# A transformer pair on one core: the second score pass of 64-wide heads over 128 contraction rows

## The chip, the cores and the metric

The kernel runs on one core of one Trainium2 chip. The metric is the device time of one execution in microseconds (us). Engines are named as in the profile: PE is TensorE's matmuls, PEld its weight loads (they can lie beside matmuls), DVE is VectorE, ACT ScalarE, POOL GpSimd, SP the queue from which nearly all DMAs are issued. The kernel before took 3671.49 us, the median of three runs between 3670.39 and 3673.18 us.

## What is computed

Two transformer blocks on 512 tokens (`S`) of 1024 features; block 2 has two layers, and its first layer also carries 256 context tokens (`C`). Both blocks have attention branches with heads of 64 features, and the change touches those:

```python
# block 1: 8 heads with a mixture of dilated windows, 8 heads on a 2-D neighbourhood, both of the form
s = einsum(q, k) * 64 ** -0.5 + bias          # masked
o = softmax(s) @ v
# block 2, in each of two layers, three branches
def mla(...):  ...                            # 8 heads of 96 features: not touched
def diff_attend(q, k, v, lam):                # 8 heads, two maps of 64 features each
    s = einsum('bqhmd,bkhmd->bhmqk', q * (DIFF_HD ** -0.5), k)
    p = softmax(s.astype(float32), axis=-1)
    a = p[:, :, 0] - lam * p[:, :, 1]
    return einsum('bhqk,bkhd->bqhd', a, v)
# sliding window with sinks: 16 query heads and 4 key heads of 64 features
p = softmax(concatenate([sink, q @ k_window, q @ k_ctx]))
# q and k of diff and of the window branch are rotated first:
def apply_rope(x, cos, sin):
    x1, x2 = halves(x)
    return concatenate([x1 * cos - x2 * sin, x2 * cos + x1 * sin])
```

Each branch is gated and merged; a feed-forward part with a short convolution ends block 1. All is in float32 accuracy.

## The kernel before

**Products in three passes.** To keep float32 accuracy, each operand of a large matmul is split into `hi` (rounded for the fast matmul mode) and `lo` (the rest), and a product is made as hi·hi + hi·lo + lo·hi. Projections do so in lines 338 to 340 and 369 to 371, the values' products in line 665, the scores of the 96-wide `mla` heads in lines 1151 to 1153. Each split costs one ACT instruction for hi and one DVE instruction for lo: `split`, lines 380 to 385. Weights are split on the way in (lines 274 and 275).

**64-wide heads.** Two heads a and b share a projection of 128 features, which stand on 128 partitions. A "page" (`hl`) is a tile of 128 partitions by 2 planes by all tokens. For queries `stack_q` builds, with three partition-to-partition DMAs from a split on 128 partitions, the planes [hi a; lo a] and [lo b; hi b]. For keys `stack_k` builds [hi a; hi a] and [hi b; hi b] with three DMAs; the keys' lo stays as it was split, a on the lower 64 partitions and b on the upper. `products` then needs two passes instead of three. Line 1158 contracts over 128 partitions: hi and lo of q with hi of k. Line 1160 is the second pass, hi of q with lo of k, and contracts over 64 partitions alone:

```python
rw = slice(64 * par, 64 * par + 64)
mm(ps, q[:, par, q_], k[:, par, k_], start=st[0], stop=False)      # L1158
mm(ps, q[rw, par, q_], kl[rw, k_], start=False, stop=st[1])        # L1160
```

**Order of the work.** The program is built by generators. `attend` emits, for each unit of a head (two tiles of 128 queries), the transposes of the unit before, then the scores and the softmax, then filling work: first the preparation of the next head (its projections, `mand`), then the gates' projections (`opt`). A scheduler of the tile framework then moves instructions within each engine's queue; it is why other matmuls stand between two score matmuls. Each engine takes its own queue in order. A matmul with 512 columns that moves at the ordinary pace starts 0.227 us after the one before it.

**Rotation.** `rope64` (line 1377) copies a projection out of PSUM (ACT, line 1386), swaps 32-row quarters with four DMAs (line 1388), multiplies on POOL and DVE and adds (lines 1389 to 1391), then splits. Context tokens are not rotated and are split straight from PSUM. Block 2 has 8 query projections of `diff` and 8 of the window branch in each layer, 32 in all, and 8 + 2 key projections in each layer, 20 in all. Block 1 has 8 query and 8 key projections with 64-wide heads.

Of the kernel before, what the change touches and what calls it, by code (L numbers as in the profile page):

```python
# [9 lines left out]
F32 = mybir.dt.float32  # L10
# [3 lines left out]
ALU = mybir.AluOpType  # L14
# [29 lines left out]
def _units():  # L44
    """Weight units in the order in which the kernel reads them: name, width, layout."""
# [103 lines left out]
def _vec_layout():  # L149
    """Columns of the per-feature vectors: name -> (first column, count)."""  # L150
# [17 lines left out]
def _consts():  # L168
    """Arrays that depend on shapes alone."""
# [9 lines left out]
    # neighbourhood masks: query p = (row, col in 16), key = (chunk, row, col in 16)  # L179
# [9 lines left out]
    # rotary tables: positions on the free axis  # L189
# [27 lines left out]
def _prep(i):  # L217
    """The arrays that are sent: inputs rearranged, and constants of the shapes."""
# [14 lines left out]
    # neighbourhood bias, [(row, col), (chunk of 16 columns - own + 1, row, head, col)] for four heads each;  # L233
    # column offsets outside of the table (all masked) repeat its edge
# [44 lines left out]
class Prog:  # L279
# [15 lines left out]
    # tiles ---------------------------------------------------------------  # L295
# [30 lines left out]
    # products ------------------------------------------------------------  # L326
# [3 lines left out]
    def load_ahead(self, names):  # L330
        """Bring in the first columns of units before the program comes to them."""
# [10 lines left out]
    def proj(self, name, x, evac, kn=KD, m=P, ctx=False, k0=0, off=0, back=False, ranges=None):  # L342
        """evac(PSUM, columns) of w^T x for m columns, x as pages. A generator: yields the tensor engine's ns."""
# [13 lines left out]
    def v_natural(self, name, x, evac, pairs, kn=KD):  # L357
        """evac(pair of token chunks, PSUM [128, 2 * 256]): tokens on partitions, 256 columns."""
# [18 lines left out]
    def split(self, dst_h, dst_l, src, scale=None):  # L377
        """hi and lo of src (times a power of two)."""
# [11 lines left out]
    # order of the program --------------------------------------------------  # L390
# [5 lines left out]
    def run_pairs(self, gens, n=2):  # L396
        """n by n, in turns: what comes in chunk by chunk is used as it comes."""
# [1337 lines left out]
```

## Time and profile before

| what | value |
|---|---|
| median of three runs | 3671.49 us |
| lowest and highest run | 3670.39, 3673.18 us |
| span of the profiled execution, first to last instruction | 3673.4 us |
| PE busy, PE loads busy | 97%, 81% of the span |
| DVE, ACT, POOL busy | 63%, 48%, 10% |
| mean granted TensorE clock | 0.985 of full speed |
| DMA engines busy, mean | about 35% |

The profiled execution has no time of its own beside its span; the span is 0.2 us above the slowest of the timed runs and 1.9 us above their median, so what lies around it is no more than that. Matmuls are pipelined: the busy time of one covers the time from its start to its modelled end, and the next one starts before that end. How fast a row of matmuls goes is therefore read from the distance between their starts, not from their durations.

### The profile page before, as it was taken

What the parts mean: (1) busy time and instruction counts of PE and PEld (TensorE: products, weight loads), DVE (VectorE), ACT (ScalarE), POOL (GpSimd) and SP (SyncE); (2) the same over time, 40 slices, a digit from 0 to 9 for tenths busy, and PEclk for the clock granted to TensorE, in tenths of its full rate; (3) what the DMA queues carried; (4) which work ended last, traced back from release to release, by engine and by line L of the source; (5) the groups of instructions that cost most, each with busy time, mean ns of one, the idle gap of its engine ahead of it and who ended that gap; (6) DMA issues with size and microseconds to landing.
All of it is one profiled execution on the core that took longest, in us unless ns stands there. A gap on an engine that the chain in (4) does not pass through costs nothing. (4 is left out here: it accounts for less than half of the span.)

```text
span 3673.4 us, 54517 instructions
## 1 busy us (share of the span) xinstructions
PE 3559.9 (97%) x19696; PEld 2968.1 (81%) x19696; DVE 2330.0 (63%) x4961; ACT 1773.1 (48%) x4102; POOL 373.0 (10%) x272
## 2 busy tenths in 40 slices
PE   6999998899999999999999999999999999999998
PEld 4777786677888898888888888888888888787777
DVE  7766689963445546556655667655565566647775
ACT  3445443333456524444434667425673444537772
POOL 3001045420001100001000001000010001000010
PEclk9999999999999999999999999999999999999999
DMA  6843455544221153222243222433114332253224
GB/s 228 260 134 111 149 165 181 176 145 133 72 65 31 44 155 81 86 70 73 65 122 126 71 63 57 126 107 88 60 50 143 100 91 77 70 166 91 72 75 138
DMA packets 203232, 396.35 MB, mean 108 GB/s; under 512 B 26865, under 2 KB 40433, under 8 KB 202962
## 3 DMA queue, kind: packets, MB, share of 16 engines
q1 hardware_dynamic: 202258, 389.17, 35.1%
q0 software_dynamic: 704, 3.70, 0.3%
q8 instruction: 155, 2.54, 0.3%
q14 instruction: 115, 0.94, 0.1%
HBM read 302.82 MB, written 38.83 MB: 93 GB/s over the span
## 5 line engine op out<-in xcount | busy, mean ns | idle before, releaser
L338 PE MATMUL mm<-h,whi 128*128 128x512 f32 (+2 forms) x2764 | 1023.2, 370 | 16.5 <-ACT whi L274 11.5
L339 PE MATMUL mm<-h,wlo 128*128 128x512 f32 (+2 forms) x2764 | 1008.2, 365 | 13.1 <-POOL wlo L275 10.5
L340 PE MATMUL mm<-h,whi 128*128 128x512 f32 (+2 forms) x2764 | 1007.7, 365 | 0.1
L274 ACT ACTIVATE whi<-wraw 128x512 fp32r<-128x512 f32 (+1 forms) x763 | 470.0, 622 | 605.9 <-PE mm L340 423.2
L275 DVE TENSOR_TENSOR wlo<-wraw,whi 128x512 fp32r<-128x512 f32 (+2 forms) x675 | 471.1, 704 | 386.8 <-ACT whi L274 376.8
L338 PEld LDWEIGHTS mm<-h,whi 128*128 128x128 f32 (+1 forms) x2764 | 529.0, 191 | 105.3 <-ACT whi L274 16.2
L339 PEld LDWEIGHTS mm<-h,wlo 128*128 128x128 f32 (+1 forms) x2764 | 529.2, 191 | 85.7 <-POOL wlo L275 15.2
L340 PEld LDWEIGHTS mm<-h,whi 128*128 128x128 f32 (+1 forms) x2764 | 528.9, 191 | 75.2 <-issue 3.4
L382 DVE TENSOR_TENSOR ptl<-t,pth 128x512 fp32r<-128x512 f32 (+1 forms) x480 | 298.5, 622 | 178.2 <-ACT pth L381 174.3
L381 ACT ACTIVATE pth<-t 128x512 fp32r<-128x512 f32 (+1 forms) x480 | 260.6, 543 | 270.2 <-PE t L647 265.8
L647 PE MATMUL t<-ident,p 128*128 128x128 f32 x1680 | 283.4, 278 | 12.5 <-DVE ptl L382 7.1
L647 PEld LDWEIGHTS t<-ident,p 128*128 128x128 f32 x1680 | 198.9, 141 | 65.4 <-DVE ptl L382 22.9
L338 PE MATMUL mm<-hl,whi 128*128 128x512 f32 (+1 forms) x680 | 241.8, 356 | 3.1 <-ACT hl L381 2.1
L339 PE MATMUL mm<-hl,wlo 128*128 128x512 f32 (+1 forms) x680 | 240.8, 354 | 0.0
L665 PE MATMUL pv<-pth,hl 128*128 128x256 f32 (+1 forms) x1184 | 223.1, 292 | 4.6 <-ACT pth L381 3.9
L665 PEld LDWEIGHTS pv<-pth,hl 128*128 128x128 f32 x1184 | 178.7, 190 | 44.0 <-ACT pth L381 27.6
L1389 POOL TENSOR_TENSOR st<-st,tab 128x512 f32<-128x512 f32 x52 | 75.1, 1445 | 1245.7 <-DMA st<-st 1034.0
L1160 PE MATMUL s<-hl,hl 64*128 64x256 f32 (+2 forms) x640 | 191.9, 372 | 0.0
L340 PE MATMUL mm<-f,whi 128*128 128x512 f32 (+1 forms) x504 | 178.4, 355 | 0.0
L1179 DVE TENSOR_REDUCE m<-s 128x1 f32<-128x512 f32 x192 | 130.3, 687 | 69.2 <-PE s L1160 52.8
L1158 PE MATMUL s<-hl,hl 128*128 128x256 f32 (+2 forms) x640 | 172.6, 342 | 1.2 <-ACT p L1557 1.2
L275 POOL TENSOR_TENSOR wlo<-wraw,whi 128x512 fp32r<-128x512 f32 x88 | 146.6, 1687 | 254.6 <-ACT whi L274 149.0
(266 smaller groups left out, 6208.5 us busy)
## 6 DMA issues: line engine op xcount, KB each, us to landing
wraw<-in_wst SPq DMA_DIRECT2D x734, 256.0 KB, 2.7
mraw<-in_w_mod SPq DMA_DIRECT2D x48, 512.0 KB, 3.7
hl<-hl SPq DMA_DIRECT2D x116, 192.0 KB, 2.8
mraw<-in_w_ada SPq DMA_DIRECT2D x36, 512.0 KB, 4.9
tg<-st SPq DMA_DIRECT2D x64, 256.0 KB, 2.0
st<-st SPq DMA_DIRECT2D x208, 64.0 KB, 2.0
hl<-hl SPq DMA_DIRECT2D x96, 128.0 KB, 2.3
p<-tg SPq DMA_DIRECT2D x40, 256.0 KB, 2.9
```

The source lines that it names most:

```text
L274: nc.scalar.activation(hi[:, :n], raw[:, :n], AF.Copy)
L275: p.lo.tensor_tensor(lo[:, :n], raw[:, :n], hi[:, :n].bitcast(F32), op=ALU.subtract)
L338: mm(ps, wh, xh, start=first, stop=False)
L339: mm(ps, wl, xh, start=False, stop=False)
L340: mm(ps, wh, xl, start=False, stop=last)
L381: nc.scalar.activation(dst_h, src, AF.Copy)
L382: nc.vector.tensor_tensor(dst_l, src, dst_h.bitcast(F32), op=ALU.subtract)
L647: self.nc.tensor.transpose(tp[:, o + i * P:o + i * P + P], pp[t][:, cols[i]:cols[i] + P], self.ident)
L665: mm(dst, sv, x_[:, o:o + w], start=first, stop=last)
L1158: mm(ps, q[:, par, q_], k[:, par, k_], start=st[0], stop=False)
L1160: mm(ps, q[rw, par, q_], kl[rw, k_], start=False, stop=st[1])
L1179: nc.vector.tensor_reduce(out=m[:, t:t + 1], in_=a[t], axis=AX.X, op=ALU.max, negate=True)
```

## The change

Queries are no longer split on 128 partitions and then moved: `put_q` writes hi and lo of each head directly where they belong, with two ACT and two DVE instructions over 64 partitions each, the DVE ones writing to the other 64 partitions than they read. For keys the lo is stacked like the hi, in a page of its own ([lo a; lo a] and [lo b; lo b]), with three more DMAs. The second pass then contracts over all 128 partitions, [hi; lo] of q with [lo; lo] of k; it so adds the product lo·lo, which was left out before.

```diff
-    def stack_q(self, pg, lp, n):
-        dma(pg[64:, 1, :n], pg[64:, 0, :n])
-        dma(pg[:64, 1, :n], lp[64:, :n])
-        dma(pg[64:, 0, :n], lp[:64, :n])
+    def put_q(self, pg, src, cs, scale):
+        for r, o, c in ((slice(0, 64), slice(64, P), 0), (slice(64, P), slice(0, 64), 1)):
+            hi = pg[r, c, cs]
+            nc.scalar.activation(hi, src[r], AF.Copy, scale=scale)
+            nc.vector.scalar_tensor_tensor(pg[o, c, cs], src[r], scale, hi.bitcast(F32), op0=ALU.mult,
+                                           op1=ALU.subtract)
-    def stack_k(self, pg, n):
+    def stack_k(self, pgs, n):
+        for pg in pgs:
+            dma(pg[64:, 1, :n], pg[64:, 0, :n])
+            dma(pg[:64, 1, :n], pg[64:, 0, :n])
+            dma(pg[64:, 0, :n], pg[:64, 0, :n])
...
     def products(self, qs, ks, jobs):
-        rw = slice(64 * par, 64 * par + 64)
...
-            mm(ps, q[rw, par, q_], kl[rw, k_], start=False, stop=st[1])
+            mm(ps, q[:, par, q_], kl[:, par, k_], start=False, stop=st[1])
...
             def ev_q(ps, cs):      # neighbours
-                hv = own(q[:, 0])
-                nc.scalar.activation(hv, fwd(ps), AF.Copy, scale=0.125)
-                for c in range(4):
-                    nc.vector.scalar_tensor_tensor(own(lo[:, 0])[:, c], fwd(ps)[:, c], 0.125, hv[:, c].bitcast(F32),
-                                                   op0=ALU.mult, op1=ALU.subtract)
-                self.stack_q(q, lo[:, 0], S)
+                qt = self.st()
+                nc.scalar.activation(own(qt), fwd(ps), AF.Copy)
+                self.put_q(q, qt, cs, 0.125)
...
-        klo = self.page()          # window branch
-        kps = [(self.page(), klo[:, g]) for g in range(2)]
+        kps = [(self.page(), self.page()) for g in range(2)]
...
-            q, lo = st["q", j], _ = self.page(), self.page()
+            q = st["q", j] = self.page()
```

The order on three engines is shown at the second `diff` head of layer 0, whose queries' page is `hl_12703` before and `hl_12719` now, the keys' hi page `hl_12704` and `hl_12720`, the keys' lo page `hl_12705` and `hl_12721`.

ACT, the conversion of that head's queries, before (line 384 writes hi on 128 partitions, of the context's 256 columns and of the 512 rotated ones):

```order
L384 ACTIVATE hl_12703<-mm_12808 128x256
L274 ACTIVATE whi_13130<-wraw_13128 128x512
L381 ACTIVATE pth_12863<-t_12858 128x512
L381 ACTIVATE pth_12872<-t_12867 128x512
L384 ACTIVATE hl_12703<-st_12796 128x512
```

The same place now (line 1132 is `put_q`'s hi; the exponentials' lines are one lower):

```order
L1132 ACTIVATE hl_12719<-mm_12826 64x256
L274 ACTIVATE whi_13150<-wraw_13148 128x512
L1132 ACTIVATE hl_12719<-mm_12826 64x256
L381 ACTIVATE pth_12880<-t_12875 128x512
L381 ACTIVATE pth_12889<-t_12884 128x512
L1132 ACTIVATE hl_12719<-st_12812 64x512 x2
```

Two instructions became four, each with as many columns as before and half the partitions; DVE's line 1133 follows them in the same way.

SP, the DMAs of the same head, before (line 1132 is `stack_q`, line 1139 `stack_k`, line 1388 the rotation's swap of the keys, line 266 weights, line 1209 a gate that is parked):

```order
L1132 DMA hl_12703<-hl_12703 64x768
L1132 DMA hl_12703<-hl_12705 64x768
L1388 DMA st_12946<-st_12945 32x512
L1132 DMA hl_12703<-hl_12705 64x768
L1388 DMA st_12946<-st_12945 32x512 x3
L266 DMA wraw_13390<-in_wst 128x512
L266 DMA wraw_13417<-in_wst 128x512
L1139 DMA hl_12704<-hl_12704 64x768 x2
L1209 DMA tg_2520_11773<-st_13039 128x512
L1139 DMA hl_12704<-hl_12704 64x768
```

The same place now (line 1138 is `stack_k`, line 1387 the swap):

```order
L1387 DMA st_12963<-st_12962 32x512 x4
L266 DMA wraw_13411<-in_wst 128x512
L266 DMA wraw_13438<-in_wst 128x512
L1138 DMA hl_12720<-hl_12720 64x768 x2
L1138 DMA hl_12721<-hl_12721 64x768 x2
L1138 DMA hl_12720<-hl_12720 64x768
L1208 DMA tg_2524_11785<-st_13059 128x512
L1138 DMA hl_12721<-hl_12721 64x768
```

The three DMAs of the queries are gone, and the swap of the keys is no longer between them; the keys have six instead of three.

PE, the second map's scores in a unit of that head, before (`mm` is a projection of values that fills; `s_13553` and `s_13554` are the scores of two query tiles with x's keys, `s_13555` those with the context's):

```order
L1158 MATMUL s_13553<-hl_12704,hl_12703 128x512
L1160 MATMUL s_13553<-hl_12705,hl_12703 128x512
L371 MATMUL mm_13477<-whi_13480,h_1080_4552 128x256
L369 MATMUL mm_13477<-whi_13583,h_1081_4553 128x256
L370 MATMUL mm_13477<-wlo_13584,h_1081_4553 128x256
L371 MATMUL mm_13477<-whi_13583,h_1081_4553 128x256
L369 MATMUL mm_13477<-whi_13583,h_1082_4554 128x256
L1158 MATMUL s_13554<-hl_12704,hl_12703 128x512
L1160 MATMUL s_13554<-hl_12705,hl_12703 128x512
L1158 MATMUL s_13555<-hl_12704,hl_12703 128x256 x2
L1160 MATMUL s_13555<-hl_12705,hl_12703 128x256 x2
```

And now (`s_13577` to `s_13579` are the same scores, lines 1157 and 1159 the two passes):

```order
L1157 MATMUL s_13577<-hl_12720,hl_12719 128x512
L1159 MATMUL s_13577<-hl_12721,hl_12719 128x512
L369 MATMUL mm_13667<-whi_13504,h_1084_4564 128x256
L370 MATMUL mm_13667<-wlo_13505,h_1084_4564 128x256
L371 MATMUL mm_13667<-whi_13504,h_1084_4564 128x256
L369 MATMUL mm_13667<-whi_13607,h_1085_4565 128x256
L370 MATMUL mm_13667<-wlo_13608,h_1085_4565 128x256
L371 MATMUL mm_13667<-whi_13607,h_1085_4565 128x256
L1157 MATMUL s_13578<-hl_12720,hl_12719 128x512
L1159 MATMUL s_13578<-hl_12721,hl_12719 128x512
L1157 MATMUL s_13579<-hl_12720,hl_12719 128x256 x2
L1159 MATMUL s_13579<-hl_12721,hl_12719 128x256 x2
```

The passes still alternate, with the same filling work between them; here the whole group stands some 22 rows later in PE's queue than before. The size at a row's end is that of the output, so the 64 contraction rows of line 1160 don't show in it.

## Rows read from the trace of the kernel before

**Rows 1.** The page: span, and busy time of the engines.

```profile
span 3673.4 us, 54517 instructions
...
PE 3559.9 (97%) x19696; PEld 2968.1 (81%) x19696; DVE 2330.0 (63%) x4961; ACT 1773.1 (48%) x4102; POOL 373.0 (10%) x272
```

**Rows 2.** What PE's matmuls waited for, the two longest: total us, times, longest.

```profile
PE mm L338 <- ACT whi L274: 11.5, 7, 3.3
PE mm L339 <- POOL wlo L275: 10.5, 13, 1.3
```

**Rows 3.** Score matmuls by form: out<-in, shape, count | busy, mean ns | idle before.

```profile
L1160 PE MATMUL s<-hl,hl 64*128 64x256 f32 x400 | 100.6, 321 | 0.0
...
L1160 PE MATMUL s<-hl,hl 64*128 64x512 f32 x160 | 72.0, 480 | 0.0
...
L1153 PE MATMUL s<-hl,hl 128*128 128x512 f32 x64 | 25.1, 398 | 0.0
...
L1153 PE MATMUL s<-hl,hl 128*128 128x256 f32 x80 | 22.7, 283 | 0.0
```

**Rows 4.** PE in order of time around scores of `diff`: start us, us, what.

```profile
1704.55 0.39 PE L339 MATMUL mm<-h,wlo 128*128 128x512 f32 x1
1704.77 0.39 PE L1158 MATMUL s<-hl,hl 128*128 128x512 f32 x1
1705.09 0.49 PE L1160 MATMUL s<-hl,hl 64*128 64x512 f32 x1
1705.51 0.50 PE L340 MATMUL mm<-h,whi 128*128 128x512 f32 x1
1705.85 0.40 PE L338 MATMUL mm<-h,whi 128*128 128x512 f32 x1
1706.09 0.40 PE L339 MATMUL mm<-h,wlo 128*128 128x512 f32 x1
```

**Rows 5.** PE in the three-pass scores of `mla`, in order of time.

```profile
1003.89 0.39 PE L1153 MATMUL s<-hl,hl 128*128 128x512 f32 x1
1004.12 0.39 PE L1152 MATMUL s<-hl,hl 128*128 128x512 f32 x1
```

**Rows 6.** PE's weight loads in the stretch of rows 4.

```profile
1704.55 0.19 PEld L1158 LDWEIGHTS s<-hl,hl 128*128 128x128 f32 x1
1705.09 0.18 PEld L1160 LDWEIGHTS s<-hl,hl 64*128 64x128 f32 x1 [0.35 <-issue]
```

**Rows 7.** All matmuls of line 1160: count, ns min/median/max, first and last start.

```profile
L1160 PE MATMUL s<-hl,hl x640: 271/381/792, 84.3 to 3555.7; 64*128 64x512 f32 x72, 64*128 64x256 f32 x64, 64*128 64x384 f32 x24
```

**Rows 8.** Line 1160 in the first stretch: length, PE busy (count), PEld busy, clock, DMA.

```profile
80.00:400.00 320.00, 29.57 (x64) 11.89 (x64) 0.98 0.55 167
```

**Rows 9.** Conversions on ACT and DVE by form.

```profile
L385 DVE SCALAR_TENSOR_TENSOR hl<-st,hl 128x512 fp32r<-128x512 f32 x32 | 21.9, 686 | 5.5 <-ACT hl L384 4.9
...
L384 ACT ACTIVATE hl<-st 128x512 fp32r<-128x512 f32 x32 | 20.2, 631 | 67.1 <-DVE st L1391 67.0
...
L382 DVE TENSOR_TENSOR hl<-mm,hl 64x512 fp32r<-64x512 f32 x16 | 11.0, 688 | 11.3 <-ACT hl L381 11.1
...
L381 ACT ACTIVATE hl<-mm 64x512 fp32r<-64x512 f32 x16 | 9.5, 593 | 14.4 <-PE mm L340 14.2
```

**Rows 10.** Two stretches: length, busy PE, PEld, DVE, ACT, POOL, clock, DMA.

```profile
80.00:400.00 320.00, 314.08 (x1524) 241.08 (x1523) 217.77 (x531) 153.69 (x336) 24.57 (x30) 0.98 0.55 167
...
3310.00:3580.00 270.00, 268.28 (x1442) 210.47 (x1441) 206.52 (x573) 196.67 (x549) 19.18 (x15) 1.00 0.27 78
```

**Rows 11.** DMAs between partitions, from the page: count, KB, us to landing.

```profile
hl<-hl SPq DMA_DIRECT2D x116, 192.0 KB, 2.8
```

**Rows 12.** The DMA queue's own waits: total us, times, longest.

```profile
SPq L266 <- DVE wlo L275: 1429.7, 514, 22.7
...
SPq L1139 <- ACT hl L381: 62.8, 20, 6.6
...
SPq L1139 <- DMA hl<-hl: 34.6, 24, 3.1
```

More of the change, by code (lines that the diff above doesn't have):

```diff
@@ L703, in prep @@
             q, k, lo = [self.page() for _ in range(3)]
-            st["q", g], st["k", g] = q, (k, lo[:, 1])
+            st["q", g], st["k", g] = q, (k, lo)
             ys.append(self.f3())
             def ev_q(ps, cs):
-                self.split(q[:, 0], lo[:, 0], ps[:, ::-1], 0.125)
-                self.stack_q(q, lo[:, 0], S)
+                self.put_q(q, ps[:, ::-1], cs, 0.125)
             def ev_k(ps, cs):
-                self.split(k[:, 0], lo[:, 1], ps)
-                self.stack_k(k, S)
+                self.split(k[:, 0], lo[:, 0], ps)
+                self.stack_k((k, lo), S)
             gens = [self.proj(f"qd{g}", h, ev_q), self.proj(f"kd{g}", h, ev_k)]
@@ L780, in prep @@
             q, k, lo = [self.page() for _ in range(3)]
-            st["q", g], st["k", g] = q, (k, lo[:, 1])
+            st["q", g], st["k", g] = q, (k, lo)
             ys.append(self.f3())
@@ L789, in ev_q @@
             def ev_q(ps, cs):
-                hv = own(q[:, 0])
-                nc.scalar.activation(hv, fwd(ps), AF.Copy, scale=0.125)
-                for c in range(4):
-                    nc.vector.scalar_tensor_tensor(own(lo[:, 0])[:, c], fwd(ps)[:, c], 0.125, hv[:, c].bitcast(F32),
-                                                   op0=ALU.mult, op1=ALU.subtract)
-                self.stack_q(q, lo[:, 0], S)
+                qt = self.st()
+                nc.scalar.activation(own(qt), fwd(ps), AF.Copy)
+                self.put_q(q, qt, cs, 0.125)
             def ev_k(ps, cs):
-                self.split(own(k[:, 0]), own(lo[:, 1]), fwd(ps))
-                self.stack_k(k, S)
+                self.split(own(k[:, 0]), own(lo[:, 0]), fwd(ps))
+                self.stack_k((k, lo), S)
             def ev_v(ps, cs):
@@ L1128, in stat_wide @@
         return stat
-    def stack_q(self, pg, lp, n):
-        dma = lambda d, s_: self.nc.sync.dma_start(d.bitcast(F32), s_.bitcast(F32))
-        dma(pg[64:, 1, :n], pg[64:, 0, :n])
-        dma(pg[:64, 1, :n], lp[64:, :n])
-        dma(pg[64:, 0, :n], lp[:64, :n])
-    def stack_k(self, pg, n):
-        dma = lambda d, s_: self.nc.sync.dma_start(d.bitcast(F32), s_.bitcast(F32))
-        dma(pg[64:, 1, :n], pg[64:, 0, :n])
-        dma(pg[:64, 1, :n], pg[64:, 0, :n])
-        dma(pg[64:, 0, :n], pg[:64, 0, :n])
+    def put_q(self, pg, src, cs, scale):
+        nc = self.nc
+        for r, o, c in ((slice(0, 64), slice(64, P), 0), (slice(64, P), slice(0, 64), 1)):
[4 more added lines that the diff above has]
+    def stack_k(self, pgs, n):
+        dma = lambda d, s_: self.nc.sync.dma_start(d.bitcast(F32), s_.bitcast(F32))
+        for pg in pgs:
+            dma(pg[64:, 1, :n], pg[64:, 0, :n])
+            dma(pg[:64, 1, :n], pg[64:, 0, :n])
+            dma(pg[64:, 0, :n], pg[:64, 0, :n])
     def products(self, qs, ks, jobs):
@@ L1375, in mla, with rope64 @@
         yield ys, opt, tg
-    def rope64(self, pg, lp, name, h, tab, scale, ctx):
+    def rope64(self, put, name, h, tab, ctx):
         nc = self.nc
@@ L1382, in ev @@
             if cs.start:
-                self.split(pg[:, 0, cs], lp[:, cs], ps, scale)
+                put(ps, cs)
                 return
@@ L1391, in ev, with rope_q, rope_k @@
             nc.vector.tensor_tensor(a, a, b, op=ALU.add)
-            self.split(pg[:, 0, cs], lp[:, cs], a, scale)
+            put(a, cs)
         return self.proj(name, h, ev, ctx=ctx)
-    def rope_q(self, pg, lp, name, h, tab, ctx):
-        yield from self.rope64(pg, lp, name, h, tab, 0.125, ctx)
-        self.stack_q(pg, lp, S + C if ctx else S)
-    def rope_k(self, pg, lp, name, h, tab):
-        yield from self.rope64(pg, lp, name, h, tab, None, True)
-        self.stack_k(pg, S + C)
+    def rope_q(self, pg, name, h, tab, ctx):
+        return self.rope64(lambda a, cs: self.put_q(pg, a, cs, 0.125), name, h, tab, ctx)
+    def rope_k(self, pg, lo, name, h, tab):
+        yield from self.rope64(lambda a, cs: self.split(pg[:, 0, cs], lo[:, 0, cs], a), name, h, tab, True)
+        self.stack_k((pg, lo), S + C)
     def rope_tab(self):
@@ L1436, in prep @@
             q, k, lo = [self.page() for _ in range(3)]
-            st["q", j], st["k", j] = q, (k, lo[:, 0])
+            st["q", j], st["k", j] = q, (k, lo)
             st["eps", j] = self.t(self.sp, [P, 8], F32, "eps", 3)
             ys.append(self.f3())
-            gens = [self.rope_q(q, lo[:, 1], f"dq{l}_{j}", h, tab, ctx), self.rope_k(k, lo[:, 0], f"dk{l}_{j}", h, tab)]
+            gens = [self.rope_q(q, f"dq{l}_{j}", h, tab, ctx), self.rope_k(k, lo, f"dk{l}_{j}", h, tab)]
             if j % 2 == 0:
@@ L1518, in prep @@
         def prep(j):
-            q, lo = st["q", j], _ = self.page(), self.page()
+            q = st["q", j] = self.page()
             ys.append(self.f3())
-            gens = [self.rope_q(q, lo[:, 0], f"sq{l}_{j}", h, tab, ctx)]
+            gens = [self.rope_q(q, f"sq{l}_{j}", h, tab, ctx)]
             if j == 0:
```

## The prediction

> **What bounds the kernel now.** I read four views, from the whole to the single matmul. First the page: PE is busy 97% of a span of 3673.4 us, DVE 63%, ACT 48% [rows 1]. Then the list of what PE waited for: the longest wait in it is 11.5 us in the whole span, the next 10.5, both for weights [rows 2]. So PE sets the end, hardly anybody keeps it waiting, and what a change is worth is the time that it takes out of or puts into PE's own row of matmuls, as long as PE stays the last.
>
> Busy PE isn't PE at its peak, so the third view is the matmuls by form. The 64-row matmuls of line 1160 last 480 ns with 512 columns and 321 ns with 256. The `mla` scores, which have the same columns and contract over 128 rows, last 398 and 283 ns [rows 3]. Half the rows take longer. Why is seen in the fourth view, PE in order of time [rows 4]. From one 512-column matmul to the next it takes 0.23 us in `mla`'s passes [rows 5], and 0.22 from the last projection matmul to line 1158. From line 1158 to the 64-row matmul it is 0.32, from that to the next 128-row one 0.42, from there 0.34, and then 0.24 again. Against 0.227 these are 0.09, 0.19, 0.11 and 0.01 us too much, 0.40 us for going into the 64-row form and out of it. No wait stands in those rows. The weight loads agree: the 128-row load for line 1158 starts at 1704.55, together with the matmul before it, while the load for line 1160 starts at 1705.09, with its own matmul, after the load unit had idled 0.35 us for nothing that the profile shows [rows 6].
>
> Line 1160 has 640 matmuls from 84.3 to 3555.7 us [rows 7]. Following PE's timeline through all of them, they stand in 352 unbroken stretches: 165 of one matmul, 127 of two, 19 of three and 41 of four. The first begins at 84.3 and the last holds the one at 3555.7. The toll is paid per stretch and not per matmul: a long stretch pays it once. Adding up, for each matmul ahead of, in and right behind such a stretch, what the distance to the next start has over the ordinary 0.227 (512 columns), 0.177 (384), 0.120 (256) or 0.109 us (128), each counted once and cut at 0.6 us so that real waits stay out, gives 142.6 us: 28.9 in block 1, where each of the 64 matmuls [rows 8] is a stretch of its own, 37.1 and 27.8 in the two `diff` branches, 22.5 and 26.3 in the two window branches. That is 0.405 us a stretch, as in rows 4; 352 times 0.40 is 141.
>
> **The change, part by part.**
>
> The second pass over 128 rows. All 640 matmuls keep their columns, and the order on PE keeps the two passes alternating, so the ordinary pace is what they cost anyway; the form is now one and the same throughout. Gone: up to 142.6 us. The trace of before has no second pass with 128 rows in these heads. Bounds from the nearest rows: at best all of 142.6 goes, since `mla` runs three 128-row passes on pages of the same kind at 0.23 [rows 5]. At the other end, if only what shows in the durations went, it would be 160 x (480 - 398) + 400 x (321 - 283) ns = 13.1 + 15.2 = 28 us [rows 3] (the 80 matmuls of 384 columns left out). I take the upper end, because the distances between starts and not the durations set the pace.
>
> Queries in place. 40 query projections (8 in block 1, 32 in block 2) have a 512-column conversion, 16 of them a 256-column one too. Each ACT and each DVE instruction becomes two over half the partitions. That saves nothing per instruction: 64x512 takes 593 ns on ACT and 688 on DVE where 128x512 takes 631 and 686 [rows 9]. ACT gets 40 more and 4 copies for the neighbourhood heads, 44 x 0.593 = 26 us, and 16 short ones, at most 10 us. DVE gets 36 x 0.688 = 25 us, the 16 short ones, at most 11 us, and in the neighbourhood heads eight instructions of 512 columns for sixteen quarters. A DVE instruction that writes to other partitions than it reads is not in these rows; between the 0.688 of its form and twice that I take 0.688. All of it lies beside PE's projections. The cover is thinnest in the last window branch: of 270 us DVE is busy 206.5 and ACT 196.7 [rows 10]. With 8 more instructions each (5.5 and 4.7 us) and PE's part shortened by about 22 us it is 212 and 201 of 248, 85% and 81%. That is still under PE's, but these engines work in chains (scores, maximum, exponential, transposes, copies), and the filling work that hides a chain goes by faster now.
>
> Fewer and other DMAs. 120 query DMAs go, 84 for the keys' lo come. A query is ready after the DVE instruction and no longer 2.8 us of landing later [rows 11]. Its extra ACT and DVE instructions cost 1.3 us, so it comes earlier. A key is ready later: the third DMA of a plane overwrites what the first two read and waits for them, and the lo's three wait for DVE as well. `stack_k` held SP's queue for 62.8 us (for ACT) and 34.6 us (for its own DMAs) over 28 keys, 3.5 us a key [rows 12]. Doubled, that is up to 97 us more on SP, less what `stack_q` held. Behind it in the queue stand weights and the rotation's swaps. The weights' loads wait 1429.7 us for a free buffer in any case [rows 12], so some microseconds of the queue are covered; and a head's keys are made first of all the filling work, one head ahead. Uncovered it can be at the start of a branch, where keys, queries and values are all still to be made: I put 3 us there. The shift of a score group by some 22 rows on PE takes nothing away, since what comes ahead of it has to be done as well.
>
> The sum. 142.6 us go. Of the 77.7 us in block 1 and the window branches, where ACT and DVE have least room, I let a tenth come back as waits, 8 us, and 3 us at the branches' starts. 3673.4 - 142.6 + 11 = 3541.8 us for the profiled span. That span is 1.9 us above the median of the runs, so the prediction is 3540 us.
>
> **The rivals.**
>
> ACT and DVE take over. In block 1 and the window branches the chain from scores to transposes becomes what PE waits for, and 60% of the 77.7 us there comes back, 47 us, and 3 at the starts: 3671.5 - 142.6 + 50 = 3579 us. For it: DVE at 76% in the last window branch before any of this. Against: PE's waits on these chains are too short to reach the top of the list now [rows 2], and block 1's stretch has DVE at 68% and ACT at 48% [rows 10].
>
> The toll isn't the rows'. If going from the first to the second pass costs what it does for another reason, such as the change of the moving operand, the 128-row pass pays it too and the change does not do what it says: 3671 us, within 0.2%. Against: `mla` changes its operand at each pass and pays nothing [rows 5], and the toll is paid again on the way out to projections [rows 4].
>
> The loads stand alone. If a 128-row load could not lie beside a running 128-row matmul, each of the 640 second passes would now show its load of 0.19 us, the length in rows 6: 640 x 0.19 = 122 us back, 3651 us. Against it: the load at 1704.55 lies wholly beside a 128-row matmul [rows 4, 6], and the 0.23 of rows 5 leaves no room for it.
> The Trainium skill states this rule (TensorE: Matmul & The Clock Gate, Part 3: Packing small matmuls — row/col tiling, on what overlaps: a weight load overlaps running matmuls only when it goes to another group of rows). By that rule the change would give 3651 us instead of 3540; the trace does not agree with it here, the load of 0.19 us costing nothing in a distance of 0.23, and the measurement decides.
>
> Slower: SP's queue. One mechanism: with six DMAs for each of the 28 keys, two of them held until others land, the queue of SP is blocked long enough that scores wait for keys or projections for weights behind them. It decides from 142.6 / 28 = 5.1 us of PE's waiting for each key. If the whole hold of a key, 2 x 3.5 us, reached PE, that is 196 us: 3671.5 - 142.6 + 196 = 3725 us. For it: a hold of up to 6.6 us has been there already [rows 12]. Against: PE's two longest waits, both for weights, come to 22 us in total over all 3673 us [rows 2], and 120 other DMAs leave the same queue.
>
> **How the numbers follow.** Forecast 0.81, within 3520 (all of the toll gone and a few us of waits with it) and 3565. ACT and DVE take over 0.12, around 3579. Toll not the rows' 0.03, 3671. Loads alone 0.01, 3651. Slower 0.03, 3725. The range reaches down to 3520 and, into the second case, up to 3580. A difference of 0.2%, 7 us, is about what can be told from none here; so faster 0.94, within 0.2% 0.03, slower 0.03.
>
> **What the profile would show.** Right: the second pass at 0.23 us from its neighbours and at about 400 and 283 ns; no loads idle for "issue" ahead of it; block 1's attention and both later branches shorter by about 29, 37, 22, 28 and 26 us; DVE about 25 to 40 us busier in all and ACT 26 to 36. Partly wrong: PE waiting for `p`, `pth` or `ptl` in the window branches, of 10 us and more. Wrong: distances of 0.3 to 0.4 us around the second pass as before, or score matmuls that wait for DMAs of `hl`.

## The result and the profile after

The changed kernel takes 3589.1 us (median of 4 runs, 3584.1 to 3592.7), the kernel before, on the same chip, 3670.9: a ratio of 0.978 (95% interval 0.976 to 0.979). It is 82 us faster; 131 were forecast, and 3589 lies above the range of 3520 to 3580.

The page of the kernel after, to be read against [rows 1]:

```profile
span 3589.2 us, 54494 instructions
...
PE 3444.7 (96%) x19696; PEld 2939.1 (82%) x19696; DVE 2368.2 (66%) x5005; ACT 1807.2 (50%) x4162; POOL 374.9 (10%) x272
```

The form that was slow is gone. The second pass of the kernel after by form (shape, count | busy, mean ns), against [rows 3]: 404 and 287 ns where it was 480 and 321.

```profile
L1159 PE MATMUL s<-hl,hl 128*128 128x256 f32 x400 | 86.6, 287 | 1.0 <-DMA hl<-hl 1.0
...
L1159 PE MATMUL s<-hl,hl 128*128 128x512 f32 x160 | 60.3, 404 | 0.0
```

PE in order of time where `diff` has one first and one second pass between projections, after, against [rows 4]:

```profile
1771.26 0.39 PE L339 MATMUL mm<-h,wlo 128*128 128x512 f32 x1
1771.48 0.39 PE L1157 MATMUL s<-hl,hl 128*128 128x512 f32 x1
1771.71 0.40 PE L1159 MATMUL s<-hl,hl 128*128 128x512 f32 x1
1771.95 0.39 PE L340 MATMUL mm<-h,whi 128*128 128x512 f32 x1
1772.18 0.40 PE L338 MATMUL mm<-h,whi 128*128 128x512 f32 x1
```

The distances are 0.22, 0.23, 0.24 and 0.23 us, where they were 0.32, 0.42 and 0.34. The loads of the same stretch stand beside the matmul before theirs; in [rows 6] that of the second pass did not:

```profile
1771.26 0.19 PEld L1157 LDWEIGHTS s<-hl,hl 128*128 128x128 f32 x1
1771.48 0.19 PEld L1159 LDWEIGHTS s<-hl,hl 128*128 128x128 f32 x1
```

So the step from which the gain was to come works as foreseen. What the gain left behind is in the load unit's list of waits over the whole span (total us, times, longest), first before, then after:

```profile
PEld s L1160 <- issue: 41.3, 155, 0.4
PEld pv L665 <- ACT pth L381: 34.4, 108, 1.0
PEld t L647 <- DVE ptl L382: 22.9, 62, 2.4
```

```profile
PEld t L647 <- DVE ptl L382: 41.6, 93, 1.6
PEld pv L665 <- ACT pth L381: 41.2, 131, 1.0
...
PEld t L647 <- ACT p L611: 15.4, 45, 1.0
```

The loads of the second pass no longer idle for "issue". Line 647 transposes a unit's probabilities, line 611 scales them, lines 381 and 382 copy the transposes out of PSUM, line 665 multiplies them with the values. PE now waits longer on the way that a unit takes through ACT and DVE.

Put into one account, by the measure of the prediction (what each distance between starts has over the ordinary pace; here nothing is cut off; PE's ordinary work is 3275.2 us in each, 11 us of the span lie ahead of its first and behind its last start, and the sums differ by just what the spans do):

| excess, us | before | after | after, but queries by DMA (e1) |
|---|---|---|---|
| at second passes (ahead, in, right behind) | 142.3 | 28.7 | 20.1 |
| at a unit's first transposes | 24.6 | 45.6 | 32.2 |
| at the values' matmuls | 36.1 | 43.8 | 44.5 |
| at projections | 102.2 | 102.2 | 105.4 |
| elsewhere | 81.9 | 82.6 | 90.2 |
| sum | 387.1 | 302.9 | 292.4 |

113.6 us went at the places of the toll; 21.0 came back at transposes, 7.7 at the values' matmuls, 0.7 elsewhere: 84.2, the difference of the spans. By stage: block 1's attention won 17 of its 29 us, the two layers' `diff` and window branches 64 of 114. The last window branch shows it best, before and after (length, busy time of PE, PEld, DVE, ACT, POOL, clock, DMA):

```profile
3203.00:3556.00 353.00, 348.40 (x1884) 280.06 (x1883) 244.37 (x638) 216.32 (x581) 25.33 (x18) 1.00 0.33 97
```

```profile
3124.00:3471.00 347.00, 334.77 (x1887) 273.93 (x1886) 252.25 (x644) 222.79 (x589) 24.64 (x18) 1.00 0.32 94
```

It is 6 us shorter, with 23.6 us of excess at its second passes before. Its idle time on PE (length less busy) rose from 4.6 to 12.2 us; so PE's 96% busy over the whole span hides it.

### The profile page after: what moved, and what is told of

The parts are those of the page before. It is cut to its first block, busy times and chain, and to the rows that moved or that the text cites. A ratio compares the mean times of both kernels' runs of the same rounds, so it can differ in the third digit from the quotient of the medians.

```text
span 3589.2 us, 54494 instructions
## 1 busy us (share of the span) xinstructions
PE 3444.7 (96%) x19696; PEld 2939.1 (82%) x19696; DVE 2368.2 (66%) x5005; ACT 1807.2 (50%) x4162; POOL 374.9 (10%) x272
## 3 DMA queue, kind: packets, MB, share of 16 engines
q1 hardware_dynamic: 199378, 385.23, 36.1%
## 5 line engine op out<-in xcount | busy, mean ns | idle before, releaser
L338 PE MATMUL mm<-h,whi 128*128 128x512 f32 (+2 forms) x2764 | 1006.1, 364 | 19.1 <-ACT whi L274 14.2
L340 PE MATMUL mm<-h,whi 128*128 128x512 f32 (+2 forms) x2764 | 1000.7, 363 | 0.1
L647 PEld LDWEIGHTS t<-ident,p 128*128 128x128 f32 x1680 | 196.3, 141 | 94.1 <-DVE ptl L382 41.6
L1184 ACT ACTIVATE p<-s,m 128x512 f32<-128x512 f32 x192 | 131.9, 687 | 89.9 <-DVE m L1179 88.1
L665 PE MATMUL pv<-ptl,hl 128*128 128x256 f32 (+1 forms) x768 | 169.2, 295 | 1.6 <-DVE ptl L382 1.5
```

What stands on the lines that cost most here:

```text
L338: mm(ps, wh, xh, start=first, stop=False)
L340: mm(ps, wh, xl, start=False, stop=last)
L647: self.nc.tensor.transpose(tp[:, o + i * P:o + i * P + P], pp[t][:, cols[i]:cols[i] + P], self.ident)
L665: mm(dst, sv, x_[:, o:o + w], start=first, stop=last)
L1184: nc.scalar.activation(p[:, 0:S], a[t], AF.Exp, bias=m[:, 2 + t:3 + t], accum_out=m[:, 4 + t:5 + t])
```

## The experiments

All ran beside the kernel before; the ratio's interval is in brackets. "Distance" is PE's own work, at the ordinary paces, that the emitted order puts between a unit's last score matmul and its first transposes (median; window branches of layer 0 / layer 1): 7.4 / 8.6 us before, 7.4 / 8.9 after, some 13 in `diff`. A run's first numbers are its median time in us, and its ratio to the kernel before. The diffs show only the lines that matter; `...` stands for the others.

**The two halves apart: e1 (keys' lo stacked and 128-row second pass, queries moved by DMA as before) and e2 (queries in place, keys' lo not stacked, 64-row second pass).**

```diff
-            mm(ps, q[rw, par, q_], kl[rw, k_], start=False, stop=st[1])       # e1, on before
+            mm(ps, q[:, par, q_], kl[:, par, k_], start=False, stop=st[1])
...
-            mm(ps, q[:, par, q_], kl[:, par, k_], start=False, stop=st[1])    # e2, on after
+            mm(ps, q[rw, par, q_], kl[rw, 0, k_], start=False, stop=st[1])
```

> The kernel before with one part of the change: the keys' lo is stacked and the second pass contracts over 128 rows, but the queries are still split on 128 partitions and moved by three DMAs. Theory A (the toll of the 64-row matmuls is gone, and in the window branches ACT's and DVE's chain from scores to transposes then sets the pace and gives most of it back): the time is that of the changed kernel, 3589 us, within 10 us. Theory B (the 60 us that are missing against the forecast were spent by the queries' extra ACT and DVE instructions): about 3540 us. Theory C (they were spent by the keys' three extra DMAs): as A, 3589 us or a little more, but then with score matmuls waiting for DMAs of hl, over 20 us in all.

> The changed kernel with the other part alone: queries are written in place by two ACT and two DVE instructions, the keys' lo is not stacked and the second pass contracts over 64 rows as before. Theory A: the extra instructions lie beside PE, 3671 us as before, within 10 us. Theory B (they cost the 60 us): 3700 us or more.

e1: 3577.2 us, 0.975 [0.973, 0.977]. e2: 3675.5 us, 1.001 [1.000, 1.002]. e1 lies just below what theory A had (3579 to 3599), and far above B; its score matmuls wait for DMAs of `hl` for 5 us in all, where theory C had over 20. Beside the toll the queries in place can't be told from nothing; with the toll gone the kernel with them is 12 us slower than the one without, and its excess at transposes is 13 us larger (45.6 against 32.2 in the table). e1 is faster than both kernels.

**Work moved off DVE: e3 (on after, weights' lo made on POOL in the window branches).**

```diff
+        self.lo = nc.gpsimd
         self.attend(heads, opt, 16 * 5200 * f)
+        self.lo = nc.vector
```

> The changed kernel with one load taken off DVE in the window branches: the lo of the weights that come in during their attention is made by POOL (48 instructions of 0.7 us on DVE in each layer, 1.7 us on POOL). Theory A: with DVE's queue freer, 10 to 30 us of the time given back come off, 3560 to 3580 us, and the second window branch is shorter by 5 to 15 us. Rivals, in which PE's own work or DMAs set the pace there: 3589 us within 5.

3617.8 us, 0.986 [0.984, 0.987]: 28 slower than after. The load unit's list of e3:

```profile
PEld t L647 <- DVE ptl L382: 67.9, 104, 3.3
```

Against 41.6 after. But the run didn't relieve DVE. It has 88 instructions less (60 us at 0.69 us each), yet by the page its busy time fell by 9 us only (2359.0 against 2368.2), since others took longer. Line 1568 scales probabilities on DVE, ahead of the transposes; by form, after and then e3:

```profile
L1568 DVE TENSOR_SCALAR p<-p,m 128x384 f32<-128x384 f32 x64 | 36.1, 563 | 0.6
L1568 DVE TENSOR_SCALAR p<-p,m 128x256 f32<-128x256 f32 x64 | 26.5, 414 | 0.5
```

```profile
L1568 DVE TENSOR_SCALAR p<-p,m 128x384 f32<-128x384 f32 x64 | 43.3, 677 | 1.0
L1568 DVE TENSOR_SCALAR p<-p,m 128x256 f32<-128x256 f32 x64 | 40.4, 631 | 0.5
```

DVE and POOL in order of time in e3 show where it comes from:

```profile
2078.16 2.82 DVE L1568 TENSOR_SCALAR p<-p,m 128x384 f32<-128x384 f32 x2
2078.17 1.29 POOL L275 TENSOR_TENSOR wlo<-wraw,whi 128x512 fp32r<-128x512 f32 x1 [12.80 <-ACT whi L274]
2079.41 1.42 POOL L1388 TENSOR_TENSOR st<-st,tab 128x512 f32<-128x512 f32 x1
```

Two scalings, of 0.42 and 0.35 us where no POOL instruction overlaps them, last 2.82 us here and end about when POOL's do. So e3 lengthened the way from the scores to the transposes, and PE's waits grew with it; it doesn't tell whether DVE's load as such is what PE waits for.

**Less and more work on PE: e4 (on after, no second pass in the window branches; the product with the keys' lo is left out there), e5 and e6 (46 us of extra matmuls, in lumps in the gates' projections of the window or of the `diff` branches), e11 and e12 (33 us, by cutting every second middle pass of these projections into 128-column pieces).**

```diff
-        for ps, q_, k_, st in jobs:
+        for ps, q_, k_, st in () if one else jobs:                            # e4
...
+                for _ in range(0 if k else dose):                             # e5, e6
+                    self.nc.tensor.matmul(ps, wh, xh[:, cs], start=True, stop=True)
...
+        for c in range(0, n, P if dose else n):                               # e11, e12
+            e = c + (P if dose else n)
+            mm(ps[:, c:e], wl, xh[:, c:e], start=False, stop=False)
```

> The changed kernel without the second pass (hi of q with lo of k) in the window branches' scores, 288 matmuls whose ordinary distances add up to 37 us of PE's work. If PE sets the pace there, 3589 - 37 = 3552 us. Theory A (ACT and DVE set it): the 37 us come back as waits for at least two thirds, 3577 us or more.

> The changed kernel with more of PE's own work among the filling projections of the window branches: each of their 16 gate projections in each layer starts with five extra 512- or 256-column matmuls whose result is overwritten. At the ordinary distances that is 27.8 us in layer 0 and 18.2 in layer 1, 46 us of PE's work and nothing for another engine. If PE's own work set the pace there, 3589 + 46 = 3635 us. Theory A2 (a unit's scores start a chain over ACT and DVE, and PE arrives at the transposes at the chain's end before it is through; so what is taken from or put into the filling work ahead of them counts only in part): at most 60% of the dose shows, 3617 us or less.

> The same dose of 46 us of PE's work in the filling projections of the two diff branches, the control. There PE's work sets the pace by either theory (the toll went almost wholly): 3589 + 46 = 3635 us, and not under 3628.

> The changed kernel with a dose for PE that is spread over the filling work of the window branches: in every second step of the gate projections one matmul of 512 or 256 columns is done in pieces of 128 columns. At the ordinary 0.109 us of a piece that adds 33 us to PE and nothing to another engine. Theory A4: the filling work is what lies beside the way over ACT and DVE, so at most 60% shows, 3609 us or less. If PE's work sets the pace: 3589 + 33 = 3622 us.

> The same spread dose of 33 us for PE in the gate projections of the diff branches. By either theory PE's work sets the pace there: 3617 to 3622 us.

e4: 3549.1 us, 0.967 [0.966, 0.969], 40 us off for 37 of work. e5: 3629.0, 0.988 [0.987, 0.990], and e6: 3628.2, 0.988 [0.986, 0.989], 40 and 39 on for 46. e11: 3661.7, 0.997 [0.996, 0.998], and e12: 3634.1, 0.990 [0.988, 0.991], 73 and 45 on for 33. I had expected the chain over ACT and DVE to hide or eat a part of each dose in the window branches. It didn't: e4's 37 us counted as 40, e5's 46 as 40, no less than in the control e6, and e11's 33 as 73, more than the 45 of the control e12. e11's list for the last window branch, then the one of after:

```profile
PEld t L650 <- ACT p L614: 21.8, 35, 1.6
PEld t L650 <- DVE ptl L385: 13.9, 35, 1.4
```

```profile
PEld t L647 <- DVE ptl L382: 11.8, 27, 1.2
PEld pv L665 <- ACT pth L381: 9.2, 34, 0.6
PEld t L647 <- ACT p L611: 5.9, 17, 1.0
```

e11 has the shorter distance, 6.6 / 6.6 us, because an edit to the work also moves the order; and its two waits at transposes together are twice those of after. e4 has 8.7 / 9.5. These doses so changed the order as well as the work, and what each of the two cost wasn't isolated.

**More PSUM banks for transposes: e7 (on e1, in the window branches every second group of transposes in a projections' bank) and e8 (everywhere).**

```diff
+            self.alt += 1
+            tp = self.ps("mm" if self.alt % 2 and self.two else "t")
```

> The kernel of the first experiment (wide second pass, queries moved by DMA; 3577 us) in which every other group of transposes of the window branches takes a PSUM bank of the projections instead of the only bank that transposes have. Theory A3 (what PE waits for at the transposes is that one bank, held until ACT's and DVE's copies of the group before are through): 10 to 25 us less, 3552 to 3567 us, and the waits of line 647 for ptl go down to a third. Rival (PE waits for the probabilities themselves, that is for the softmax): 3577 us within 5, with the same waits for p.

> As the run before, but in all branches with attention. Theory A3: some us less still, since block 1 and the diff branches have such waits too, though fewer: 3545 to 3567 us. Rival: taking a bank from the projections makes them wait where PE is the bound: 3577 us or more.

e7: 3587.0 us, 0.977 [0.975, 0.978], 10 slower than e1. e8: 3679.1, 1.002 [1.001, 1.003], 102 slower. The load unit's waits ahead of transposes in the first window branch (1925 to 2257 us), e1 and then e7, where line 649 is e1's 647 and `mm` stands for the transposes in a projections' bank:

```profile
PEld t L647 <- DVE ptl L382: 10.2, 19, 1.4
PEld t L647 <- ACT p L611: 8.0, 30, 0.6
```

```profile
PEld mm L649 <- ACT p L612: 10.6, 16, 1.2
...
PEld mm L649 <- DVE p L1573: 3.6, 7, 0.8
```

The wait for `ptl`, the copy that empties the one bank, is gone in that stretch; PE waits for the probabilities themselves instead. Over both window branches the excess ahead of transposes, in whichever bank, rose from 24 to 39 us and that ahead of scores from 5 to 14, while projections stayed under 4 and the values' matmuls fell from 18 to 9. So the bank wasn't what ended last: the rival that PE waits for the softmax has the cause, though not the time. The distance fell too (6.5 / 7.3, against 7.4 / 8.6 in e1), and what that cost wasn't isolated. In e8, over the whole span and against e1, the excess grew by 40 us ahead of transposes, by 32 ahead of scores and by 10 ahead of projections.

The Trainium skill advises that groups of matmuls that don't depend on each other go round different PSUM banks, so that the copies of one lie beside the matmuls of the next (Perfetto Trace Analysis, Optimizing Tensor Performance, Matmuls). The trace of e7 agrees as to the copies; the time doesn't, 10 us longer in a kernel that has all eight banks given out already (three each to projections and scores, one each to transposes and values).

**A longer way on DVE: e9, e10 (on after, the context's maximum taken twice in the window or the `diff` branches), e13 (the same on before, window), e14 (on e1, window), e15 (e14, and block 1's biased maximum twice).**

```diff
+                for _ in range(2):
                     nc.vector.tensor_reduce(out=m[:, 2:4], in_=cv, axis=AX.X, op=ALU.max, negate=True)
```

> The changed kernel with a dose for DVE: in the window branches the maximum over the context's scores is taken twice, 80 more reductions of 0.69 us that stand between scores and exponentials, 55 us for DVE and nothing for PE. Theory A4 (in the window branches the way from a unit's scores over ACT and DVE to its transposes is as long as PE's work beside it, so each such piece of the way shows): at least 60% of it, 3622 us or more. If PE's work sets the pace and the way has room: under 20%, 3600 us or less.

> The same dose of 80 reductions, 55 us for DVE, between scores and exponentials of the diff branches. Theory A4 says that there PE has more filling work beside each unit and the way has room: at most 35% of it shows, 3608 us or less. If DVE's total load were what counts, both doses would cost the same.

> The kernel before, with the context's maximum taken twice in the window branches (the same 55 us more on DVE as in the run where the changed kernel became 12 us faster by it). A5 (what counts is how much of PE's own work its fixed order puts between a unit's last score matmul and its first transposes; the doubled maximum moves that order): the toll of the 64-row passes already stretches this distance, so there is little to win: between -3 and +10 us against before. Rival B (the doubled maximum or the order it brings is worth 12 us for a reason that has nothing to do with the toll): the same -12 us here. Rival C (DVE's load in the window branches is what PE waits for): slower by 20 us or more.

> 128-row second pass, queries still moved by DMA, and the context's maximum taken twice in the window branches. A5: the waits at the transposes of the window branches shrink, so under the 3577 us of the same kernel without the second maximum: 3558 to 3571. B: the same 12 us, 3565. C (load of DVE): over 3585. The distance of PE's own work between scores and transposes goes by the emitted orders from 7.4 / 8.6 us (layers 0 and 1) to 8.8 / 9.2.

> As the run before, and in block 1 the biased scores' instruction that also gives the maximum done twice too (0.5 us more on DVE for each of its units). A5: block 1's distance goes from 8.3 to 8.6 us only, while its way through DVE gets longer, so the same or up to 8 us slower than the run before. C: slower by 20 us or more.

e9: 3576.7 us, 0.974 [0.973, 0.976]: 12 faster than after, though DVE got 55 us more of instructions and is busy 32 us more by the page (2400.6 against 2368.2); A4 had 3622 or more. e10: 3599.2, 0.980 [0.979, 0.982], 10 slower. e13: 3678.0, 1.002 [1.001, 1.003], 6 slower than before. e14: 3579.0, 0.975 [0.973, 0.976], and e15: 3578.0, 0.974 [0.972, 0.976], against 3577.2 of e1 no difference, with DVE busy 32 and 67 us more (2353.2 and 2388.1 against 2321.6). The list of e9 for the last window branch:

```profile
PEld pv L665 <- ACT pth L381: 19.1, 63, 0.6
PEld t L647 <- DVE ptl L382: 5.5, 19, 0.9
PEld t L647 <- ACT p L611: 2.5, 7, 0.5
```

The distance grew to 8.9 / 11.0 us, and the transposes' waits of 11.8 and 5.9 fell to 5.5 and 2.5, while that at the values grew from 9.2 to 19.1. In distances between starts, over both window branches, some 16 us went at transposes and 7 came at the values. That DVE's load sets the time falls with e9, e14 and e15. That the distance alone does falls with e14: 8.8 / 9.2 us there, and nothing won.

**A longer distance without work: e16 (on e1, a unit's scores emitted ahead of the transposes of the unit before it, in the window branches). A shorter way: e17 (on e1, the scaling of the probabilities left out in the window branches), e18 (e16 and e17 together).**

```diff
+                if self.swap:                                                 # e16, e18
+                    s_()
                 next(vals, None)
-                s_()
+                if not self.swap:
+                    s_()
...
-                    self.scale_rows(pp[t][:, S:], r)                          # e17, e18; with the latent part's
```

> 128-row second pass, queries still moved by DMA, no added work anywhere; in the window branches a unit's scores are put ahead of the transposes of the unit before it instead of behind. The distance between a unit's scores and its transposes grows to 8.1 / 11.9 us of PE's own work. A5: the waits at the transposes shrink without any more work on DVE: 3550 to 3572 against 3577. Rival C or D (the copies of a unit's transposed probabilities now queue behind the next unit's softmax on DVE, and PE waits there): slower than 3577, by 10 us or more.

> 128-row second pass, queries still moved by DMA; in the window branches the multiplication of the probabilities by one over their sum is left out (two instructions each on DVE and ACT a unit, 0.44 and 0.50 us each, some 2.9 us of work a unit and between 1.0 and 1.9 us of its way from scores to transposes; the output isn't divided). The order adapts: PE's own work between scores and transposes shrinks from 7.4 / 8.6 to 5.9 / 6.4 us. A5 (the distance less the way decides): the two nearly cancel, 3570 to 3595 against 3577. A6 (the way alone, that is the time that ACT and DVE need for a unit): faster by 15 us or more, 3562 or less. A7 (the distance alone): slower by over 20 us.

> As the run before, with a unit's scores put ahead of the transposes of the unit before it. By the emitted order PE's own work between scores and transposes is 7.5 / 8.5 us, that of the kernel with 128-row passes and queries by DMA (7.4 / 8.6), while a unit's way is 1.0 to 1.9 us shorter. A5 and A6: of the some 27 us that this kernel's waits at transposes and value matmuls have over those of before, most goes: 3550 to 3565. A7 (the distance alone): 3577 within 8 us.

e16: 3574.5 us, 0.974 [0.972, 0.975], 3 under e1 and not told apart from it. e17: 3563.6, 0.970 [0.969, 0.972], 14 under. It lies between what A5 and A6 had for it, next to A6. e18: 3567.1, 0.971 [0.970, 0.973], 10 under, a little short of what both theories had for it. The lists for the last window branch, e16 and then e17:

```profile
PEld pv L669 <- ACT pth L382: 24.9, 77, 0.5
PEld t L651 <- DVE ptl L383: 7.9, 13, 1.2
```

```profile
PEld pv L665 <- ACT pth L381: 8.0, 20, 1.3
PEld t L647 <- DVE ptl L382: 6.0, 22, 0.9
...
PEld t L647 <- ACT p L1557: 1.2, 4, 0.4
```

With a longer distance the wait goes on from the transposes to the values' matmuls. With a shorter way it gets less at both (e1 has 10.5 and 9.4 there), although e17 has the shortest distance of all (5.9 / 6.4 us). In the same account, `diff` and window branches together have 176.0 us of excess before, 100.0 in e1, 96.5 in e16, 80.5 in e17 and 88.0 in e18. So what came back are waits for a unit's way through ACT and DVE: work taken out of that way takes them off, by 14 us of time in e17. How much PE's own work beside the way counts is not shown: A5 (the distance less the way) had e16 win and e17 stand still, and by the way alone (A6) the longer way of e14 and e15 should have cost time. e17 also takes work off ACT and DVE, and no run shortens the way without that.

One place where that way is held up is seen in DVE's order in the last window branch, after:

```profile
3381.95 0.15 DVE L1560 TENSOR_TENSOR m<-m 128x2 f32<-128x2 f32 x1
3382.02 0.55 DVE L1544 CUSTOM_DVE_ANT_0 p<-s,wmask 128x384 f32<-128x384 f32 x1
...
3382.84 0.15 DVE L1562 TENSOR_TENSOR m<-m 128x2 f32<-128x2 f32 x1
3382.91 0.68 DVE L1547 TENSOR_REDUCE m<-s 128x2 f32<-128x512 f32 x1
3383.51 0.15 DVE L1563 RECIPROCAL m<-m 128x2 f32<-128x2 f32 x1
```

ACT and then PE of the same stretch:

```profile
3383.75 0.91 ACT L611 ACTIVATE p<-p,m 128x256 f32<-128x256 f32 x2 [0.48 <-DVE m L1563]
```

```profile
3384.32 0.33 PE L647 MATMUL t<-ident,p 128*128 128x128 f32 x1 [0.57 <-ACT p L611]
```

Lines 1560, 1562 and 1563 end one unit's softmax; between them stand lines 1544 and 1547 of the next unit, 0.82 and 0.60 us. The reciprocal comes late, ACT idles 0.48 us for it, and PE 0.57 for ACT. DVE isn't full there (252 of 347 us); there the reciprocal stands behind work of the next unit. No run changed this order alone, so its price is open.

## Why the prediction was wrong

**The toll goes with the 64-row form: right.** The distances are ordinary, the loads lie beside matmuls, no load idles for "issue" ahead of a second pass. The rivals "not the rows'" (3671 us) and "loads alone" (3651) fall with the timeline above. The Trainium skill says that changing the tiling mode drains TensorE (TensorEngine Tiling (Array Packing), Key Properties). A toll per stretch and not per matmul would agree with that, if the 64-row form is such a mode, which no run here shows.

**"142.6 us go": over-sized by 29.** 113.6 us went. At these places 28.7 stay in the kernel after. 15.5 of it stands in 13 distances that are over 0.4 us too long: real waits, three ahead of scores, most of the rest ahead of projections and of line 546 (sums over features), right behind a second pass. The kernel before had 5 such distances, 2.5 us, so these waits came up with the change. Another 11.8 stands in some 140 distances that are 0.05 to 0.13 too long. They look like the one here (loads, then PE, after):

```profile
3093.17 0.19 PEld L1157 LDWEIGHTS s<-hl,hl 128*128 128x128 f32 x1 [0.39 <-ACT p L1184]
```

```profile
3093.17 0.50 PE L1157 MATMUL s<-hl,hl 128*128 128x512 f32 x1
3093.51 0.39 PE L1159 MATMUL s<-hl,hl 128*128 128x512 f32 x1
```

A load that starts late and so together with its own matmul makes the next start 0.34 us away and not 0.23, in 128-row form too. The step at fault is the one that adds up all excess around a stretch and lets all of it go. 113.6 / 352 is 0.32 us a stretch net, where one clean place showed 0.40 [rows 4]. Whether late loads were in the 142.3 already, or came up when the toll no longer covered them, the runs don't say. The prediction's split of layer 1, 27.8 and 26.3, was taken by stretches of time; by branch it is 30.0 and 23.6, which changes nothing in the sum.

**"I let a tenth come back as waits, 8 us", and 3 at the branches' starts: under-sized by 18, and the step whose reason failed.** 29.4 us came back: 21.0 at transposes, 7.7 at the values and 0.7 elsewhere. With the 13 us of new waits at the second passes it is 42 against 11. The argument was that PE's list of waits showed almost none on these chains [rows 2]. That list has only what exceeds a matmul's modelled end. The distances had 24.6 us at transposes before, and the load unit's list 22.9 us for `ptl`; both stood in the trace, and I read neither. In the window branches the toll had also been time in which ACT and DVE went on; that this is why the waits grew is argued from the account, and no run puts the time back without the 64-row form. The forecast said what would take its place ("PE waiting for `p`, `pth` or `ptl` in the window branches, of 10 us and more"), and gave it 0.12.

**"Queries in place: all of it lies beside PE's projections", so nothing: wrong by 12 us.** The instructions cost what was forecast: 64x512 on DVE 686 ns, though it writes to other partitions, and DVE is 38 us busier in all, ACT 34 (forecast 25 to 40 and 26 to 36).

```profile
L1133 DVE SCALAR_TENSOR_TENSOR hl<-st,hl 64x512 fp32r<-64x512 f32 x72 | 49.4, 686 | 7.9 <-ACT hl L1132 5.6
```

With the toll there was room for them (e2: no difference), without it not (after against e1). Cover was counted by busy share (85% of DVE in the last window branch), while these instructions stand in the same queues as the softmax and the copies. That their delay there makes up the 12 us was not isolated: the emitted order changed as well, and e9, with 80 instructions more in DVE's queue, is back at e1's time.

**SP's queue: right that it costs little.** `stack_k` holds the queue somewhat longer for its own DMAs, 53.6 us against 34.6 [rows 12], and scores wait for `hl` by DMA for 1.0 us in all:

```profile
SPq L1138 <- ACT hl L381: 58.0, 19, 7.9
SPq L1138 <- DMA hl<-hl: 53.6, 43, 4.8
```

The rival "ACT and DVE take over" (3579 us) had the nearest time and the right mechanism. That it came so near is partly luck: it let 50 us come back where 29 did, and had the toll 29 too large. It missed the queries' share.

**Open.** What the doubled maximum did to win 12 us in the kernel after, when neither it (e14) nor the swapped emission (e16) wins on e1: it brings after to where e1 is, so it may undo what the queries in place did to the order; that was not isolated. And e1's window branches, each taken from the last second pass of the branch before it to its own last, got 14 us shorter, with 46 us of excess at their second passes before; leaving out the scaling takes off another 16, and the rest wasn't traced.

The fastest kernel here that leaves nothing out is e16, with e1 and e9 within 3 us of it and not told apart; e16 and e1 have the wide second pass and keep the queries' DMAs.

## What to carry to other kernels

Before a toll on the bounding engine is priced as gain, look at what runs under it: from each stage's toll take off the time by which the next engine's chain would then be late. Read that lateness from the distances between starts and from the load unit's waits, not from the matmuls' list, and read cover for added instructions from the queue in which they stand, not from a busy share. Take the two halves of a change apart: here one half was free only as long as the other hadn't been done. And when work is moved to another engine to test a load, look first whether the load fell.

## What was not expected of the hardware

A 128-row load that starts together with its own matmul, and not beside the one before, goes with a next start about 0.09 to 0.11 us late (0.34 against 0.23 in the lines above); with the 64-row matmul of [rows 4] it was 0.42. A DVE instruction that writes to the other 64 partitions takes 686 ns, as one that doesn't. DVE instructions can last far longer beside POOL's: in the window branches of e3 line 1568 took 1035 ns in the mean with POOL beside it (27 with 384 columns) and 415 without, while line 382, which reads PSUM, took 686 beside POOL and 688 without. Small changes of work move the order that is fixed when the kernel is built, and the time moved by more than the work, or the other way: 33 us of matmuls cost 73 us in one place (e11), and 55 us of DVE's instructions went with 12 us less in another (e9).
